# A hybrid decoder step: history products queued behind the adding transfers, the pooling group's newest columns ahead of VectorE's difference, two pooling products earlier

## Chip, core and metric

The kernel runs on one core of one Trainium2 chip. The metric is device time in microseconds (us), the median of several executions. All five engines of the core are used: TensorE (PE in the profile; PEld is its weight load), VectorE (DVE), ScalarE (ACT), GpSimd (POOL) and SyncE (SP, which only issues transfers).

## What is computed

One inference step of one hybrid layer on 288 token columns: 256 columns of a new sequence (the prompt) and 8 x 4 new columns of running requests (the samples). All in float32, channels on the partitions.

```
h    = RMSNorm(x)                                  # D_MODEL = 2048
a, gate, z = split(h @ w_in + b_in)                # 1024 columns each
u    = a * sigmoid(gate)
c    = silu(LayerNorm(depthwise_conv31(history ++ u)))
d    = windowed_mean(history ++ z) - z             # windows 2, 4, 8, 16, one for each of 4 groups
p    = (d @ pool_w, per group) * pool_scale
x   += concat(c, p) @ w_out
x   += relu(RMSNorm(x) @ w_ff1)^2 @ w_ff2          # D_FF = 8192
y    = RMSNorm(x)
```

The outputs are y for prompt and samples and the new convolution and pooling histories.

## The kernel before, in words

**Split products.** Every matrix product is made of three TensorE passes. A weight tile `wr` (128 x 1024 float32, 512 KB) is loaded, ScalarE rounds it to `whi` (line 260), and the rest `wlo = wr - whi` is made in one of three ways, which the table `WAYS` (line 73) deals out in turn: "V" on VectorE (line 265), "G" on GpSimd in two halves (line 268), and "D" by a transfer: ScalarE writes `-whi` into `wlo` (line 262), and a DMA issued from GpSimd's queue adds the weight to it straight from memory (line 263). These are the adding transfers; there are seven, in the stages that the code calls c3, c4, p3 and c5. The activations are split the same way (`hx`, `dx`, `mx`, `ax`, `fx`). A weight tile serves 24 matmuls; five pairs of `whi`, `wlo` buffers rotate, so a tile's cast waits for TensorE to be done with the tile five before it.

**Stages.** `SEQUENCE` (line 45) sets the order of the work on TensorE: eight convolution blocks c0 to c7 (128 channels of a and gate each, 96 matmuls of 128x128 on 128x288), four input blocks of the pooling groups p3 to p0, and the small pooling products P3 to P0 (12 matmuls each, line 498, into the accumulator `pp`). Then comes the output projection w0 to w7, first over the pooling half and then over the convolution half, and last the two feed-forward products, which take most of the time.

**Beside TensorE.** When a convolution block's accumulator is full, `conv_pair` (lines 426 to 461) scales it on VectorE (line 432), makes the gate on ScalarE (line 434) and u on VectorE (line 436). The 31 taps of the prompt columns are a chain of VectorE instructions (line 448); two blocks' chains alternate. The taps of the sample columns are one GpSimd product per block over the history windows (line 451, tile `prd`, 128 x 992 elements, the history product) and one VectorE reduction (line 453). These are recorded with a late priority, so a scheduler lays them into the gaps that it sees. It sets each engine's order once, when the program is built; on the chip every engine takes its queue strictly in that order.

For a pooling group, `pool_group` (lines 465 to 491) scales the accumulator on VectorE (line 470, tile `tz`), adds the bias on ScalarE into `z_all`, makes running sums `s` on GpSimd by doubling (line 479), corrects the first sums (line 483), and forms `d`: VectorE for the 256 prompt columns (line 484), then GpSimd for the 32 newest, sample columns, a scaling of `s` in place (line 486) and a difference (line 487). ScalarE rounds d to `dx` hi (line 489) and VectorE makes `dx` lo (line 490). The pooling products read both.

**Orders written out by hand.** In a matmul group, each pair of row blocks gives six matmuls: four with hi activations (two with `whi`, two with `wlo`), then two with lo activations. `classes` (line 317) can deal the first matmuls of a group out in another order; the string `TURN` (line 70) is given to c2, c5, the start of w0 and some later groups. `between` (line 324) puts something into a group: in c7 the products P1 stand in front of row block 12 of 16, and in the shared group of w0 and w1 the products P0 stand in front of pair (0, 2), that is behind 36 matmuls.

Of the kernel before, what the change touches and what calls it, by code (L numbers as in the profile page):

```python
# [12 lines left out]
ALU = mybir.AluOpType  # L13
# [3 lines left out]
P = 128  # L17
D = 2048
SEQ = 256
NB, NS = 8, 4  # L20
# [4 lines left out]
CW = 31  # L25
# [61 lines left out]
def trunk_kernel(ctx: ExitStack, tc: tile.TileContext, io):  # L87
# [46 lines left out]
    def f32(t):  # L134
        return t.bitcast(F32)
# [113 lines left out]
        last = mm(psum[:, 0, :T], minus, total, start=True, stop=True)  # L249
        return row_of(psum, psum[:, 0, :T], *args), last  # L250

    turns = {}

    def split_part(raw, src, hi, lo, way):

        nc.scalar.copy(hi, raw)  # L260
        if way == "D":
            nc.scalar.activation(lo, f32(hi), AF.Copy, scale=-1.0)
            nc.gpsimd.dma_start(lo, src, accum_op=ALU.add)
        elif way == "V":
            nc.vector.tensor_tensor(lo, raw, f32(hi), op=ALU.subtract)  # L265
        else:
            for j in range(0, raw.shape[1], 2):
                nc.gpsimd.tensor_tensor(lo[:, j : j + 2, :], raw[:, j : j + 2, :], f32(hi[:, j : j + 2, :]), op=ALU.subtract)  # L268

    def spl():  # L270
        return [wspl.tile([P, 4, 256], F32R, name=nm("w" + part), tag="w" + part) for part in ("hi", "lo")]
# [140 lines left out]
    rb = row("rb")  # L412


    cs, pcs = [], []
    sum_c = tmpp.tile([P, 2, T], F32, name="sum_c", tag="ag2", bufs=2)

    def history(i):
# [8 lines left out]
    def conv_pair(i, banks):  # L427
        up = u_all[:, i, 0:UO]
        us = samples(u_all[:, i, UO:UL], US)
        ta, gate = [b[:, :T] for b in banks]  # L430
        for b in (gate, ta):
            nc.vector.tensor_tensor(b, b, rb, op=ALU.mult)
        tg = tmpp.tile([P, 2, T], F32, name=nm("tg"), tag="ag", bufs=2)[:, 0, :]
        nc.scalar.activation(tg, gate, AF.Sigmoid, bias=v("b_in", 8 + i))
        for out, a, b in ((up[:, CH:UO], ta[:, :SEQ], tg[:, :SEQ]), (us[:, :, CH:US], samples(ta[:, SEQ:T], NS), samples(tg[:, SEQ:T], NS))):
            nc.vector.scalar_tensor_tensor(out=out, in0=a, scalar=v("b_in", i), in1=b, op0=ALU.add, op1=ALU.mult)
        if i % 2 == 0:
            cs.append(actp.tile([P, 2, T], F32, name=nm("c"), tag="c", bufs=4))
        c = cs[i // 2][:, i % 2, :]
        with later():  # L440
            if i % 2 == 0:
                pcs.append(cvp.tile([P, 2, SEQ], F32, name=nm("pc"), tag="cv"))
            pc = pcs[i // 2][:, i % 2, :]
            cwv = vec[:, CWO + i * CW : CWO + (i + 1) * CW]
            nc.scalar.activation(pc, up[:, 0:SEQ], AF.Identity, bias=v("conv_b", i), scale=cwv[:, 0:1])  # L445
            for w in range(1, CW):
                dst = pc if w < CW - 1 else c[:, 0:SEQ]
                nc.vector.scalar_tensor_tensor(out=dst, in0=up[:, w : w + SEQ], scalar=cwv[:, w : w + 1], in1=pc, op0=ALU.mult, op1=ALU.add)  # L448
            prd = prdp.tile([P, NB, NS, CW + 1], F32, name=nm("prd"), tag="prd")
            nc.scalar.activation(prd[:, :, :, CW], ones[:, 0 : NB * NS].rearrange("p (b t) -> p b t", t=NS), AF.Identity, bias=v("conv_b", i), scale=0.0)  # L450
            nc.gpsimd.tensor_tensor(prd[:, :, :, 0:CW], windows(us, CW), cwv[:, None, None, :].to_broadcast([P, NB, NS, CW]), op=ALU.mult)  # L451
            cso = c[:, SEQ:T]
            nc.vector.tensor_reduce(samples(cso, NS), prd, axis=AX.X, op=ALU.add)
            if i % 2 and 1 < i < N8 - 1:
                for m in range(2):
                    nc.gpsimd.tensor_tensor(sum_c[:, m, :], (cs[0] if i == 3 else sum_c)[:, m, :], cs[i // 2][:, m, :], op=ALU.add)
            if i == N8 - 2:
                for part in (sum_c[:, 1, :], c):
                    nc.gpsimd.tensor_tensor(sum_c[:, 0, :], sum_c[:, 0, :], part, op=ALU.add)
# [4 lines left out]
    def pool_group(g):  # L464
        nc.sync.dma_start(z_all[:, 2 * g : 2 * g + 2, ZO:ZL], io["hist_p"][:, 2 * g : 2 * g + 2, :])
        bk = bank2()
        gemm(each(bk), hx)
        z = z_all[:, 2 * g : 2 * g + 2, :]
        tz = tmpp.tile([P, 2, T], F32, name=nm("tz"), tag="ag", bufs=2)
        nc.vector.tensor_tensor(tz, bk[:, :, :T], both(rb), op=ALU.mult)  # L470
        for m in range(2):
            b_in = v("b_in", 16 + 2 * g + m)
            nc.scalar.activation(z[:, m, PH:ZO], tz[:, m, 0:SEQ], AF.Identity, bias=b_in)
            nc.scalar.activation(samples(z[:, m, ZO:ZL], ZS)[:, :, PH:ZS], samples(tz[:, m, SEQ:T], NS), AF.Identity, bias=b_in)
        s, w = z, 1
# [8 lines left out]
        nc.vector.scalar_tensor_tensor(out=d[:, :, 0:SEQ], in0=s[:, :, PH:ZO], scalar=1.0 / w, in1=z[:, :, PH:ZO], op0=ALU.mult, op1=ALU.subtract)  # L484
        news = [x[:, :, ZO:ZL].rearrange("p m (b t) -> p m b t", t=ZS)[:, :, :, PH:] for x in (s, z)]
        nc.gpsimd.tensor_scalar(news[0], news[0], 1.0 / w, None, op0=ALU.mult)
        nc.gpsimd.tensor_tensor(d[:, :, SEQ:T].rearrange("p m (b t) -> p m b t", t=NS), news[0], news[1], op=ALU.subtract)
        dh, dl = act2("dx", tag="p", bufs=4)
        nc.scalar.copy(dh, d)
        nc.vector.tensor_tensor(dl, d, f32(dh), op=ALU.subtract)  # L490
        dd[g] = dh, dl
# [33 lines left out]
    for kind, i in SEQUENCE[3:-1]:  # L525
        if (kind, i) == ("P", 1):
            continue
        if kind == "c":
            conv_pair(i, conv_products(i, classes=TURN if i == 5 else "", **(dict(gets=ahead(1), between={12: lambda: pool_products(1)}) if i == 7 else {})))
        elif kind == "p":  # L530
            pool_group(i)
        else:
            pool_products(i)
    proj = [halves(dd[k // 2])[k % 2] for k in korder]
    bks = [bank2() for _ in range(2)]
    both_gets = [ahead(1) for _ in range(2)]
    early = [(k, m) for k in (0, 2, 4) for m in range(4)]
    early.sort(key=lambda km: km[1] // 2)
    gemm(each(bks[0]) + each(bks[1]), proj, gets=[lambda k, m: both_gets[m // 2][0](k, m % 2)], between={(0, 2): lambda: pool_products(0)}, classes="." * 36 + TURN, pairs=early + [(6, m) for m in range(4)])
    chain.clear()  # L540
    load_table(AF.Abs_reciprocal_sqrt, f32(mixp[1][0])[:, 0:1])
    with later(2 * LATER):
# [239 lines left out]
```

## Time and profile before

| | |
|---|---|
| median of 3 runs | 1081.95 us (1081.67 to 1083.03) |
| the profiled execution's own time | 1082.43 us |
| its span, first to last instruction | 1080.6 us |
| busy: TensorE, VectorE, ScalarE, GpSimd | 1069.2, 633.7, 479.0, 175.9 us |
| matmuls | 8176 |
| granted TensorE clock | 0.998 |

The profile is of one execution. The 1.8 us between its time and its span lie outside the first and the last instruction. Times of day in the trace are microseconds from the span's start. GpSimd works almost only in the first 205 us, which hold the mixing part of the layer; the change touches nothing behind it. An engine's idle time is put down to whatever released it last.

### The profile page before, as it was taken

To read this page: it belongs to the slowest core of one execution; us is meant where nothing else is said; L and a number is where in the kernel's file an instruction comes from. 1 tells how busy PE (TensorE), PEld (TensorE's weight loads), DVE (VectorE), ACT (ScalarE), POOL (GpSimd) and SP (SyncE) were. 2 spreads that over 40 slices of the span, in tenths; PEclk is the share of its full clock that TensorE was granted. 3 is DMA by queue.
4 is the path that set the end of the run, shared out by engine and by line. 5 is a ranking of instruction groups with operands and counts; after the bars stand their busy time and mean duration, and the time that the engine had idled before them with its cause. 6 is when DMAs were issued, how large, how long until landed. Compare 5 with 4: busy or idle time off the path is not lost.

```text
span 1080.6 us, 19528 instructions
## 1 busy us (share of the span) xinstructions
PE 1069.2 (99%) x8176; PEld 1067.9 (99%) x8176; DVE 633.7 (59%) x810; ACT 479.0 (44%) x588; POOL 175.9 (16%) x182
## 2 busy tenths in 40 slices
PE   9999999999999999999999999999999999999996
PEld 8999999999999999999999999999999999999996
DVE  7899999788654544444554444555544445554553
ACT  8654445665544433334443333444433334444441
POOL 0878979512000000000000000000000000000001
PEclk9999999999999999999999999999999999999999
DMA  9896478555555555555555555555555555555522
GB/s 326 288 263 182 145 187 247 177 171 173 162 173 166 169 175 163 170 173 165 170 174 164 170 170 167 171 173 162 173 168 167 173 171 164 173 166 170 172 79 88
DMA packets 58296, 190.71 MB, mean 176 GB/s; under 512 B 6240, under 2 KB 11232, under 8 KB 58208
## 3 DMA queue, kind: packets, MB, share of 16 engines
q1 hardware_dynamic: 56336, 184.35, 54.3%
q0 software_dynamic: 1008, 3.67, 1.9%
q8 instruction: 64, 1.05, 0.4%
q10 hardware_dynamic: 864, 1.44, 0.4%
q14 instruction: 24, 0.20, 0.0%
HBM read 185.16 MB, written 4.28 MB: 175 GB/s over the span
## 4 chain that ended last, share of the span: by engine, by line
PE 75%; issue 21%; ACT 2%; POOL 1%; DMA 1%; SPq 0%; POOLq 0%; DVE 0%
PE ac L291 74%; POOL wlo L268 1%; DMA wr<-in_w 1%; ACT whi L349 1%; PE pp L291 1%; DMA wlo<-in_w 1%; ACT hx L354 0%; ACT z_all L405 0%; POOL prd L451 0%; POOL xT L718 0%; ACT whi L260 0%; SPq L191 0%; POOLq L768 0%; DVE xT L691 0%; ACT whi L356 0%
## 5 line engine op out<-in xcount | busy, mean ns | idle before, releaser
L260 ACT CAST whi<-wr 128x1024 fp32r<-128x1024 f32 (+1 forms) x332 | 346.5, 1044 | 551.3 <-PE ac L291 536.7
L265 DVE TENSOR_TENSOR wlo<-wr,whi 128x1024 fp32r<-128x1024 f32 x288 | 353.5, 1227 | 348.1 <-ACT whi L260 348.1
L291 PE MATMUL ac<-ax,whi 128*128 128x288 f32 x2048 | 351.0, 292 | 0.0
L291 PE MATMUL ac<-fx,whi 128*128 128x288 f32 x2048 | 350.2, 292 | 0.0
L291 PEld LDWEIGHTS ac<-ax,whi 128*128 128x128 f32 x2048 | 296.0, 187 | 0.0
L291 PEld LDWEIGHTS ac<-fx,whi 128*128 128x128 f32 x2048 | 295.6, 187 | 0.0
L291 PE MATMUL ac<-ax,wlo 128*128 128x288 f32 x1024 | 217.3, 292 | 0.0
L291 PE MATMUL ac<-fx,wlo 128*128 128x288 f32 x1024 | 216.4, 292 | 0.0
L291 PEld LDWEIGHTS ac<-ax,wlo 128*128 128x128 f32 x1024 | 162.5, 187 | 0.0
L291 PEld LDWEIGHTS ac<-fx,wlo 128*128 128x128 f32 x1024 | 162.2, 187 | 0.0
L291 PE MATMUL ac<-hx,whi 128*128 128x288 f32 x768 | 131.9, 296 | 1.4 <-DVE hx L352 1.4
L718 POOL TENSOR_TENSOR xT<-xT,rf 128x288 f32<-128x288 f32 x4 | 3.1, 795 | 799.9 <-ACT rf L722 799.9
L291 PEld LDWEIGHTS ac<-hx,whi 128*128 128x128 f32 x768 | 112.6, 190 | 1.8 <-ACT hx L354 1.7
L268 POOL TENSOR_TENSOR wlo<-wr,whi 128x512 fp32r<-128x512 f32 x74 | 102.4, 1433 | 17.1 <-ACT whi L260 16.0
L448 DVE SCALAR_TENSOR_TENSOR pc<-u_all,vec,pc 128x256 f32<-128x256 f32 x232 | 99.3, 479 | 1.9 <-ACT pc L445 0.7
L291 PE MATMUL ac<-hx,wlo 128*128 128x288 f32 x384 | 80.4, 295 | 0.2 <-DMA wlo<-in_w 0.2
L291 PEld LDWEIGHTS ac<-hx,wlo 128*128 128x128 f32 x384 | 61.1, 189 | 0.4 <-DMA wlo<-in_w 0.4
L291 PE MATMUL ac<-dx,whi 128*128 128x288 f32 x256 | 46.8, 295 | 0.0
L291 PE MATMUL ac<-mx,whi 128*128 128x288 f32 x256 | 44.9, 293 | 0.0
L660 DVE SCALAR_TENSOR_TENSOR t<-ac,r 128x576 f32<-128x576 f32 x32 | 24.2, 757 | 25.4 <-PE ac L291 25.3
L291 PEld LDWEIGHTS ac<-dx,whi 128*128 128x128 f32 x256 | 38.4, 188 | 0.2
L291 PEld LDWEIGHTS ac<-mx,whi 128*128 128x128 f32 x256 | 37.5, 188 | 0.2 <-DVE xT L579 0.2
(129 smaller groups left out, 529.6 us busy)
## 6 DMA issues: line engine op xcount, KB each, us to landing
wr<-in_w SPq DMA_DIRECT2D x335, 512.0 KB, 3.8
wlo<-in_w POOLq DMA_DIRECT2D x7, 512.0 KB, 7.8
xT<-in_xT SPq DMA_DIRECT2D x8, 288.0 KB, 7.7
wr<-in_w SPq DMA_DIRECT2D x5, 256.0 KB, 3.9
out_u_out<-u_all SPq DMA_DIRECT2D x1, 1208.0 KB, 9.6
u_all<-in_hist_c SPq DMA_DIRECT2D x8, 136.0 KB, 5.3
out_z_out<-z_all SPq DMA_DIRECT2D x1, 668.0 KB, 9.2
z_all<-in_hist_p SPq DMA_DIRECT2D x4, 152.0 KB, 6.6
```

The costliest lines, as they stand in the source:

```text
L260: nc.scalar.copy(hi, raw)
L265: nc.vector.tensor_tensor(lo, raw, f32(hi), op=ALU.subtract)
L268: nc.gpsimd.tensor_tensor(lo[:, j : j + 2, :], raw[:, j : j + 2, :], f32(hi[:, j : j + 2, :]), op=ALU.subtract)
L291: last = nc.tensor.matmul(*args, **kw)
L349: nc.scalar.copy(hi[:, blocks[0]], raw[:, blocks[0]])
L448: nc.vector.scalar_tensor_tensor(out=dst, in0=up[:, w : w + SEQ], scalar=cwv[:, w : w + 1], in1=pc, op0=ALU.mult, op1=ALU.add)
L660: nc.vector.scalar_tensor_tensor(out=t, in0=bk[:, :, :T], scalar=0.0, in1=both(rows2[0]), op0=ALU.max, op1=ALU.mult)
L718: eng.tensor_tensor(xk, xk, r[:, None, :].to_broadcast([P, n, T]), op=ALU.mult)
```

## The change

Four edits, all of them on the order of work; every operation, its size and its count stay.

1. The history product of a block is recorded so that it stands behind an adding transfer in GpSimd's queue: blocks 0 and 1 behind the first transfer, block 2 behind the second, blocks 3 and up behind the fourth. For this the taps of blocks 2 and 3 are recorded one block later.
2. In a pooling group GpSimd's two operations on the newest columns are recorded ahead of VectorE's difference. They work in place on `s`, so before, the scaling had to wait for VectorE to have read it.
3. From c7 on, the weight differences on GpSimd stand behind group 1's newest columns, and those of the output projection behind group 0's.
4. P1 goes in front of row block 8 of c7 instead of 12 (24 matmuls sooner), and P0 in front of pair (4, 0), behind 24 matmuls instead of 36. `TURN` follows P0 as before.

```diff
-            nc.gpsimd.dma_start(lo, src, accum_op=ALU.add)
+            added.append(nc.gpsimd.dma_start(lo, src, accum_op=ALU.add))
...
-                nc.gpsimd.tensor_tensor(lo[:, j : j + 2, :], raw[:, j : j + 2, :], f32(hi[:, j : j + 2, :]), op=ALU.subtract)
+                with tc.issue_after(pooled[-1].ins) if pooled else nullcontext():
+                    nc.gpsimd.tensor_tensor(lo[:, j : j + 2, :], raw[:, j : j + 2, :], f32(hi[:, j : j + 2, :]), op=ALU.subtract)
...
+        while waiting:
+            taps(*waiting.pop())
+        if i in (2, 3):
+            waiting.append((i, up, us))
+        else:
+            taps(i, up, us)
...
-            nc.gpsimd.tensor_tensor(prd[:, :, :, 0:CW], windows(us, CW), cwv[:, None, None, :].to_broadcast([P, NB, NS, CW]), op=ALU.mult)
+            with tc.issue_after(added[max(0, min(3, 2 * i - 3))].ins):
+                nc.gpsimd.tensor_tensor(prd[:, :, :, 0:CW], windows(us, CW), cwv[:, None, None, :].to_broadcast([P, NB, NS, CW]), op=ALU.mult)
...
-        nc.vector.scalar_tensor_tensor(out=d[:, :, 0:SEQ], in0=s[:, :, PH:ZO], scalar=1.0 / w, in1=z[:, :, PH:ZO], op0=ALU.mult, op1=ALU.subtract)
...
-        nc.gpsimd.tensor_tensor(d[:, :, SEQ:T].rearrange("p m (b t) -> p m b t", t=NS), news[0], news[1], op=ALU.subtract)
+        last = nc.gpsimd.tensor_tensor(d[:, :, SEQ:T].rearrange("p m (b t) -> p m b t", t=NS), news[0], news[1], op=ALU.subtract)
+        newest[g] = last
+        nc.vector.scalar_tensor_tensor(out=d[:, :, 0:SEQ], in0=s[:, :, PH:ZO], scalar=1.0 / w, in1=z[:, :, PH:ZO], op0=ALU.mult, op1=ALU.subtract)
...
+        if i == 7:
+            pooled.append(newest[1])
-            ... between={12: lambda: pool_products(1)} ...
+            ... between={8: lambda: pool_products(1)} ...
...
+    pooled.append(newest[0])
-    gemm(..., between={(0, 2): lambda: pool_products(0)}, classes="." * 36 + TURN, ...)
+    gemm(..., between={4: lambda: pool_products(0)}, classes="." * 24 + TURN, ...)
```

Two places show what this does to the queues. First GpSimd's queue around the first adding transfer, in stage c3: `wlo_609` is the tile that the transfer adds to, the two `prd` are the history products of blocks 0 and 1, the other `wlo` are weight differences of c2 and c3. Before:

```order
L268 TENSOR_TENSOR wlo_604<-wr_599,whi_603 128x512 x2
L451 TENSOR_TENSOR prd_667<-u_all,vec 128x32x31
L451 TENSOR_TENSOR prd_708<-u_all,vec 128x32x31
L263 DMA wlo_609<-in_w 128x1024
L268 TENSOR_TENSOR wlo_618<-wr_613,whi_617 128x512 x2
```

And now:

```order
L269 TENSOR_TENSOR wlo_604<-wr_599,whi_603 128x512 x2
L263 DMA wlo_609<-in_w 128x1024
L462 TENSOR_TENSOR prd_667<-u_all,vec 128x32x31
L462 TENSOR_TENSOR prd_708<-u_all,vec 128x32x31
L269 TENSOR_TENSOR wlo_618<-wr_613,whi_617 128x512 x2
```

The transfer now leaves ahead of both products. The second and the fourth transfer change places with one product each in the same way.

The other place is VectorE's queue around the difference of pooling group 1 (`d_1868`, its lo part `dx_1873`), which P1 reads. The `pc` rows are taps, the `wlo` rows weight differences, `tz_2023` is the next group's scaling. Before, with `tz_2023` in the row right ahead of these:

```order
L484 SCALAR_TENSOR_TENSOR d_1868<-s_1865,z_all 128x2x256
L448 SCALAR_TENSOR_TENSOR pc_1057<-u_all,vec,pc_1057 128x256
L448 SCALAR_TENSOR_TENSOR pc_1714<-u_all,vec,pc_1714 128x256
L265 TENSOR_TENSOR wlo_2064<-wr_2056,whi_2063 128x1024
L448 SCALAR_TENSOR_TENSOR pc_1057<-u_all,vec,pc_1057 128x256
L448 SCALAR_TENSOR_TENSOR pc_1714<-u_all,vec,pc_1714 128x256
L265 TENSOR_TENSOR wlo_2157<-wr_2154,whi_2156 128x512
L448 SCALAR_TENSOR_TENSOR pc_1057<-u_all,vec,pc_1057 128x256
L448 SCALAR_TENSOR_TENSOR pc_1714<-u_all,vec,pc_1714 128x256
L448 SCALAR_TENSOR_TENSOR pc_1057<-u_all,vec,pc_1057 128x256
L448 SCALAR_TENSOR_TENSOR pc_1714<-u_all,vec,pc_1714 128x256
L490 TENSOR_TENSOR dx_1873<-d_1868,dx_1873 128x2x288
```

And now:

```order
L499 SCALAR_TENSOR_TENSOR d_1868<-s_1865,z_all 128x2x256
L458 SCALAR_TENSOR_TENSOR pc_1057<-u_all,vec,pc_1057 128x256
L458 SCALAR_TENSOR_TENSOR pc_1714<-u_all,vec,pc_1714 128x256
L458 SCALAR_TENSOR_TENSOR pc_1057<-u_all,vec,pc_1057 128x256
L458 SCALAR_TENSOR_TENSOR pc_1714<-u_all,vec,pc_1714 128x256
L458 SCALAR_TENSOR_TENSOR pc_1057<-u_all,vec,pc_1057 128x256
L502 TENSOR_TENSOR dx_1873<-d_1868,dx_1873 128x2x288
L458 SCALAR_TENSOR_TENSOR pc_1714<-u_all,vec,pc_1714 128x256
L458 SCALAR_TENSOR_TENSOR pc_1057<-u_all,vec,pc_1057 128x256
L481 TENSOR_TENSOR tz_2023<-ac_1920,rb_250 128x576
L458 SCALAR_TENSOR_TENSOR pc_1714<-u_all,vec,pc_1714 128x256
L458 SCALAR_TENSOR_TENSOR pc_1057<-u_all,vec,pc_1057 128x256
```

Between the difference and its lo part stand five taps, where eight taps and two weight differences stood; `tz_2023`, ahead of both before, and the weight differences now follow. Counted from the second result of P2 (line 502, `dx_1536`), 26 taps, `tz_2023` and two weight differences stood ahead of `dx_1873`; now 11 taps do.

On TensorE the 12 matmuls of P1 and the 12 of P0 move as edit 4 says, and nothing else does but the dealing by `TURN` behind P0, which now begins one pair earlier.

More of the change, by code (lines that the diff above doesn't have):

```diff
@@ L250, in row_of_sums @@
         return row_of(psum, psum[:, 0, :T], *args), last
-    turns = {}
+    turns, added, newest, pooled = {}, [], {}, []
     def split_part(raw, src, hi, lo, way):
@@ L412, in trunk_kernel @@
     rb = row("rb")
-    cs, pcs = [], []
+    cs, pcs, waiting = [], [], []
     sum_c = tmpp.tile([P, 2, T], F32, name="sum_c", tag="ag2", bufs=2)
@@ L438, in conv_pair, with taps @@
             cs.append(actp.tile([P, 2, T], F32, name=nm("c"), tag="c", bufs=4))
+        while waiting:
[4 more added lines that the diff above has]
+            taps(i, up, us)
+    def taps(i, up, us):
         c = cs[i // 2][:, i % 2, :]
@@ L527, in trunk_kernel @@
             continue
+        if i == 7:
+            pooled.append(newest[1])
         if kind == "c":
-            conv_pair(i, conv_products(i, classes=TURN if i == 5 else "", **(dict(gets=ahead(1), between={12: lambda: pool_products(1)}) if i == 7 else {})))
+            conv_pair(i, conv_products(i, classes=TURN if i == 5 else "", **(dict(gets=ahead(1), between={8: lambda: pool_products(1)}) if i == 7 else {})))
         elif kind == "p":
@@ L538, in trunk_kernel @@
     early.sort(key=lambda km: km[1] // 2)
-    gemm(each(bks[0]) + each(bks[1]), proj, gets=[lambda k, m: both_gets[m // 2][0](k, m % 2)], between={(0, 2): lambda: pool_products(0)}, classes="." * 36 + TURN, pairs=early + [(6, m) for m in range(4)])
+    gemm(each(bks[0]) + each(bks[1]), proj, gets=[lambda k, m: both_gets[m // 2][0](k, m % 2)], between={4: lambda: pool_products(0)}, classes="." * 24 + TURN, pairs=early + [(6, m) for m in range(4)])
     chain.clear()
```

## The prediction

> **What bounds the kernel now.** I read the page first, then who TensorE waits for, then its timeline around the waits.
>
> ```profile
> PE 1069.2 (99%) x8176; PEld 1067.9 (99%) x8176; DVE 633.7 (59%) x810; ACT 479.0 (44%) x588; POOL 175.9 (16%) x182
> ```
>
> ```profile
> PE ac L291 <- DVE hx L352: 1.4, 1, 1.4
> PE ac L291 <- DMA wlo<-in_w: 0.2, 1, 0.2
> ```
>
> TensorE is the bound, and the list of its waits is nearly empty: 1.4 us at the start, which the change does not reach, and one wait for an adding transfer. The change cannot shorten TensorE's work; all it can win is what TensorE loses between matmuls. The timeline of TensorE around that one wait (start, length, what, how many) shows more than the 0.2 us of the list:
>
> ```profile
> 47.99 0.68 PE L291 MATMUL ac<-hx,whi 128*128 128x288 f32 x4
> ...
> 48.77 0.68 PE L291 MATMUL ac<-hx,whi 128*128 128x288 f32 x4
> ...
> 49.55 0.68 PE L291 MATMUL ac<-hx,whi 128*128 128x288 f32 x4
> 50.42 0.54 PE L291 MATMUL ac<-hx,wlo 128*128 128x288 f32 x2 [0.20 <-DMA wlo<-in_w]
> 50.80 0.69 PE L291 MATMUL ac<-hx,whi 128*128 128x288 f32 x4
> ...
> 52.39 0.70 PE L291 MATMUL ac<-hx,whi 128*128 128x288 f32 x4
> ...
> 53.19 0.70 PE L291 MATMUL ac<-hx,whi 128*128 128x288 f32 x4
> ```
>
> Ahead of the wait six matmuls take 0.78 us (48.77 to 49.55), 130 ns each. Four of these from 49.55 should bring the next at 50.07; it came at 50.42, 0.35 late. The two behind it took 0.38 instead of 0.26, another 0.12. And from there six take 0.80 (52.39 to 53.19), 133.3 ns each. That lasts until c5, where the order `TURN` breaks the pattern of four and two:
>
> ```profile
> 85.19 0.56 PE L291 MATMUL ac<-hx,whi 128*128 128x288 f32 x3
> ```
>
> The windows show the slow stretch and a later one at a full clock (the columns: stretch, length, busy and matmuls, granted clock, DMA share, GB/s):
>
> ```profile
> 51.00:84.00 33.00, 33.00 (x250) 1.00 0.95 256
> 95.00:128.00 33.00, 33.00 (x256) 1.00 0.49 152
> ```
>
> Six matmuls fewer in 33 us. Is the slower spacing the wait's doing? A second place says so: later TensorE waits a little once more (a group of four takes 0.90 instead of 0.68), and again six take 0.80 behind it.
>
> ```profile
> 219.19 0.90 PE L291 MATMUL ac<-mx,whi 128*128 128x288 f32 x4
> ...
> 220.19 0.69 PE L291 MATMUL ac<-mx,whi 128*128 128x288 f32 x4
> ...
> 220.99 0.70 PE L291 MATMUL ac<-mx,whi 128*128 128x288 f32 x4
> ```
>
> **The first adding transfer leaves earlier.** GpSimd's and ScalarE's timelines, and the transfer in the chain of waits:
>
> ```profile
> 38.90 1.30 POOL L268 TENSOR_TENSOR wlo<-wr,whi 128x512 fp32r<-128x512 f32 x1
> 40.16 4.33 POOL L451 TENSOR_TENSOR prd<-u_all,vec 128x992 f32<-128x992 f32 x2
> 44.41 1.01 POOL L263 DMA_DIRECT2D wlo<-in_w  x1
> ```
>
> ```profile
> 39.26 1.06 ACT L262 ACTIVATE wlo<-whi 128x1024 fp32r<-128x1024 f32 x1
> ```
>
> ```profile
> 44.41 5.97 DMA wlo<-in_w
> ```
>
> What the transfer needs, ScalarE's negated tile, is ready at 40.32 and GpSimd's difference ahead of it ends at 40.20; it then stands behind two history products for 4.1 us. Ahead of them it leaves at about 40.4 and, with the same 5.97 us, lands at 46.4, against 50.07 when TensorE wants it: 3.7 us to spare. So the wait goes. Gain: 0.35 + 0.12, and the slow spacing from 50.80 to 85.2: 34.4 / 0.1333 = 258 matmuls at 3.3 ns, 0.86. Sum **1.33 us**.
>
> [...]
>
> The moved products cost: both wait for the transfer's issue, at most 1.0 us of GpSimd, and end that much later than before. Behind them on GpSimd stand c3's weight differences, which start no later, since issue and products only change places. VectorE, in strict order, reaches its two reductions and waits there for some 1 us in all, with the taps and c2's scaling queued behind. VectorE's cover is its own wait for TensorE:
>
> ```profile
> DVE ac L432 <- PE ac L291: 2.5, 3, 1.3
> ```
>
> Three waits, 2.5 us in all, the longest 1.3. I cost it at nothing; without that cover it would be 1 us of taps, late on an engine that TensorE does not wait for until the layer norm.
>
> **The later adding transfers come close.** Once TensorE is faster, the next transfers are due sooner. By 76 us it is 0.47 + 0.63 = 1.1 us early, by 79 us 1.18. The tightest are the fourth and the fifth, in stage p3: issue, time to landing, and the weight load that needs the tile.
>
> ```profile
> 63.76 2.16 POOL L451 TENSOR_TENSOR prd<-u_all,vec 128x992 f32<-128x992 f32 x1
> 65.99 0.88 POOL L263 DMA_DIRECT2D wlo<-in_w  x1
> 68.90 0.87 POOL L263 DMA_DIRECT2D wlo<-in_w  x1 [2.04 <-ACT wlo L262]
> ```
>
> ```profile
> wlo<-in_w POOLq DMA_DIRECT2D x1, 512.0 KB, 9.8
> ```
>
> ```profile
> wlo<-in_w POOLq DMA_DIRECT2D x1, 512.0 KB, 10.2
> ```
>
> ```profile
> 75.99 0.32 PEld L291 LDWEIGHTS ac<-hx,wlo 128*128 128x128 f32 x2
> ```
>
> ```profile
> 79.19 0.32 PEld L291 LDWEIGHTS ac<-hx,wlo 128*128 128x128 f32 x2
> ```
>
> ```profile
> 64.38 1.06 ACT L262 ACTIVATE wlo<-whi 128x1024 fp32r<-128x1024 f32 x1
> ```
>
> The fourth lands at 65.99 + 9.8 = 75.8, wanted at 75.99; the fifth at 68.90 + 10.2 = 79.1, wanted at 79.19. Hardly any room. The fourth no longer stands behind a history product (63.76 to 65.92): its negated tile is ready at 65.44, and that cast is paced by TensorE, 0.8 us earlier, so it leaves at about 64.9, 1.1 us sooner, and keeps its 0.2 us. The fifth waits for ScalarE, 0.86 us earlier by the same pacing, while it is due 1.18 earlier: short by 0.2 if it still takes 10.2 us. But the 10.2 are a queue: the two land 3.3 us apart, and the one ahead starts 1.1 us sooner. Bounds: no wait at all, or a landing that does not move (79.1 against 78.0), a wait of 1.1 us with 0.12 and some 45 slow matmuls (0.15) behind it, which eats the gain. I take none, since both the queue ahead and the issue move forward, and keep 0 to 1.3 for the range.
>
> **The pooling part.** P1 is wanted 24 matmuls, 3.12 us, sooner, and TensorE is 1.33 us early. Its fifth matmul reads the lo part:
>
> ```profile
> 160.94 0.68 PE L291 MATMUL pp<-dx,whi 128*128 128x288 f32 x4
> ```
>
> ```profile
> 148.60 3.22 DVE L448 SCALAR_TENSOR_TENSOR pc<-u_all,vec,pc 128x256 f32<-128x256 f32 x8
> ...
> 152.41 1.35 DVE L484 SCALAR_TENSOR_TENSOR d<-s,z_all 128x512 f32<-128x512 f32 x1
> ...
> 154.47 1.69 DVE L265 TENSOR_TENSOR wlo<-wr,whi 128x1024 fp32r<-128x1024 f32 x1
> ...
> 159.03 0.75 DVE L490 TENSOR_TENSOR dx<-d,dx 128x576 fp32r<-128x576 f32 x1
> ```
>
> ```profile
> 156.87 0.86 POOL L487 TENSOR_TENSOR d<-s,z_all 128x64 f32<-128x64 f32 x1
> ```
>
> Before, it ended at 159.78, wanted at 160.94. Now it is wanted at 156.5, so it must come 3.3 us sooner. Since P2's second result 15 taps at about 0.39 (3.22 for 8, overlapping by 0.08) and two weight differences, the larger 1.6, no longer stand ahead of it: at least 7.5 us less. The rows printed around it account for three taps and the larger difference, 2.8 us, with the smaller one and `tz` on top, and VectorE is packed here, so fewer rows ahead is sooner. What else it needs, GpSimd's newest columns, stood behind weight differences until 157.73 and now stands ahead of them. That puts three small operations, the largest 0.86 here, at most 2.6 us, in front of GpSimd's weight tiles for c7:
>
> ```profile
> 145.50 5.05 POOL L268 TENSOR_TENSOR wlo<-wr,whi 128x512 fp32r<-128x512 f32 x4
> ```
>
> ```profile
> 151.19 0.32 PEld L291 LDWEIGHTS ac<-hx,wlo 128*128 128x128 f32 x2
> ```
>
> The first of these two tiles is done halfway, at 148.0, and wanted at 151.19: 3.2 us, and since their casts are paced by TensorE, its earliness does not shorten that. The cover holds; without it the loss would be what is late, 2.6 at most. Nothing is won on TensorE by being sooner either: gain and cost nothing. P0 reads its lo part in the same way:
>
> ```profile
> 170.30 0.68 PE L291 MATMUL pp<-dx,whi 128*128 128x288 f32 x4
> ```
>
> ```profile
> 165.42 0.74 DVE L490 TENSOR_TENSOR dx<-d,dx 128x576 fp32r<-128x576 f32 x1
> ```
>
> It ended at 166.16 (165.42 and 0.74) and was wanted at 170.30. It is now wanted 1.56 (12 matmuls) and 1.33 sooner, which leaves 1.2 us even if VectorE gains nothing.
>
> **The sum.** The profiled execution took 1082.43, 1.8 more than its span and 0.48 over the median of the three runs, 1081.95. 1082.43 - 1.33 = 1081.10 for such an execution, and 1081.95 - 1.33 = **1080.6** for the median.
>
> **Rivals.**
>
> (1) A later adding transfer takes over the wait. For it: the 0.1 to 0.2 us of room; against: it leaves sooner. Typically a wait of 0.25 with 0.27 behind it: 1080.6 + 0.5 = 1081.1; at the bound 1081.9. Chance 0.22.
>
> (2) [...] Chance 0.10.
>
> (3) P1 becomes the wait, and the kernel slower. If VectorE's lo part of group 1 stays where it was in time, because ScalarE or GpSimd hold up its difference and all taps behind it, TensorE stands 3.3 us at P1, then 0.12, then runs slow for about 84 matmuls until `TURN` (0.28): +3.7 - 1.33 = 2.4, 1084.3. It decides when VectorE moves forward by less than 3.3 us; the rows printed around it give 2.8 and a little more, the whole count 7.5. Chance 0.06.
>
> (4) The wait stays: the landing hangs on the DMA engines rather than on the issue (share 0.95 in that stretch). Against: 4 us sooner. 1081.95. Chance 0.04.
>
> (5) The short wait at 219 us goes as well, as everything ahead of it shifts: another 0.22 and, if the slow spacing there lasts 10 us, 75 matmuls at 3.3 ns (0.25): 1080.1. Nothing in the change is aimed there. Chance 0.06.
>
> The forecast keeps 0.52.
>
> **How the numbers follow.** From 1079.9 (rival 5, and 0.2 of spread between medians) to 1082.2 (rivals 1 and 4 at their bound, and 0.25 of the same spread) lie all cases but rival 3 and tails. About 0.2% (2.2 us) is what a measurement of this kernel tells from no change. Faster by more than that needs over 2.2 us, more than the forecast and rival 5 together (1.8): 0.04. Slower by that much is rival 3: 0.06. Within: 0.90.
>
> **What would show it.** Right: the transfer leaves at about 40.4, TensorE's list has no wait for `wlo`, six matmuls take 0.78 from 43 to 85 us, the window 51 to 84 holds 256 matmuls, c7 starts 1.3 us sooner, and P1 follows without a gap. Wrong: a wait for `wlo` at 75 to 79 us (rival 1), 0.80 for six without a wait ahead of it (rival 2), a wait for `dx` at 156 (rival 3).

## The result and the profile after

| | median of its runs | ratio to before, 95% interval |
|---|---|---|
| before | 1082.35 us (7 runs) | |
| changed | 1085.95 us (7 runs) | 1.0031 [1.0021, 1.0042] |

The kernel became slower by 3.6 us, more than the 0.2% that the prediction set as the bound. The profiled execution took 1085.72 us, its span is 1084.0.

**The first adding transfer did what was forecast.** GpSimd's timeline shows it leaving at 40.75 (it stood at 44.41), and TensorE's timeline runs through the place of the old wait without a gap, six matmuls in 0.78 us (start, length, what, how many):

```profile
40.75 1.05 POOL L263 DMA_DIRECT2D wlo<-in_w  x1 [0.74 <-POOL wlo L269]
```

```profile
49.35 0.68 PE L292 MATMUL ac<-hx,whi 128*128 128x288 f32 x4
...
50.13 0.68 PE L292 MATMUL ac<-hx,whi 128*128 128x288 f32 x4
...
61.83 0.68 PE L292 MATMUL ac<-hx,whi 128*128 128x288 f32 x4
62.58 0.53 PE L292 MATMUL ac<-hx,wlo 128*128 128x288 f32 x2
62.95 0.69 PE L292 MATMUL ac<-hx,whi 128*128 128x288 f32 x4
...
63.74 0.70 PE L292 MATMUL ac<-hx,whi 128*128 128x288 f32 x4
```

Two things in the lower rows: at 62.58 a new gap. The four matmuls from 61.83 should bring the next at 62.35; it came 0.23 late and two more took 0.37 instead of 0.26. It is the second adding transfer, which I had not worked out, and behind it the spacing is slow again (62.95 to 63.74: six in 0.79 to 0.80).

**The loss is at 165 us.** TensorE's timeline there, then the granted clock in two windows (stretch, length, busy and matmuls, clock, DMA share, GB/s):

```profile
164.45 0.42 PE L292 MATMUL ac<-dx,whi 128*128 128x288 f32 x2
167.00 0.53 PE L292 MATMUL ac<-dx,wlo 128*128 128x288 f32 x2 [2.12 <-DVE wlo L265]
167.37 0.69 PE L292 MATMUL ac<-dx,whi 128*128 128x288 f32 x4
...
168.23 1.16 PE L292 MATMUL ac<-dx,whi 128*128 128x288 f32 x4
169.19 0.68 PE L292 MATMUL ac<-dx,wlo 128*128 128x288 f32 x2
```

```profile
164.60:168.00 3.40, 1.27 (x10) 1.00 0.79 145
168.10:171.40 3.30, 3.30 (x16) 0.50 0.98 382
```

TensorE stands from 164.7 to 167.0 for the first weight tile of w0 (way "V", line 265); two matmuls take 0.26, so 2.29 are lost. Then the clock is at 0.50 for 3.4 us: four matmuls take 0.96 (168.23 to 169.19), 240 ns each, and with some 14 of them another 1.5 us go. 2.29 + 0.11 (the two behind the wait) + 1.5 = 3.9. Against that stand 0.45 us won between 46 and 151 us, and 0.2 by which this execution started up sooner. Net 3.25; the two profiled executions differ by 3.29. The profiled execution has two such stretches at half clock, the other at its start (7.6 us), and a mean clock of 0.995. Three of the seven executions have 0.997, by the same count room for only one, so the 1.5 us need not be in each of them.

The late tile itself, on VectorE's timeline after and before:

```profile
165.72 1.23 DVE L265 TENSOR_TENSOR wlo<-wr,whi 128x1024 fp32r<-128x1024 f32 x1
```

```profile
163.00 1.28 DVE L265 TENSOR_TENSOR wlo<-wr,whi 128x1024 fp32r<-128x1024 f32 x1
```

**Why VectorE is late.** VectorE's and GpSimd's timelines in stage p0, after and, below, before:

```profile
133.81 2.29 DVE L265 TENSOR_TENSOR wlo<-wr,whi 128x1024 fp32r<-128x1024 f32 x1
...
137.97 2.22 DVE L265 TENSOR_TENSOR wlo<-wr,whi 128x1024 fp32r<-128x1024 f32 x1
```

```profile
132.46 2.55 POOL L269 TENSOR_TENSOR wlo<-wr,whi 128x512 fp32r<-128x512 f32 x2
137.83 3.52 POOL L269 TENSOR_TENSOR wlo<-wr,whi 128x512 fp32r<-128x512 f32 x2 [2.82 <-ACT whi L260]
```

```profile
133.53 1.21 DVE L265 TENSOR_TENSOR wlo<-wr,whi 128x1024 fp32r<-128x1024 f32 x1
...
136.23 1.21 DVE L265 TENSOR_TENSOR wlo<-wr,whi 128x1024 fp32r<-128x1024 f32 x1
```

```profile
131.76 4.13 POOL L268 TENSOR_TENSOR wlo<-wr,whi 128x512 fp32r<-128x512 f32 x2
```

The same differences took 1.21 us before and 2.29 and 2.22 after. GpSimd's pair that began at 132.46 ends at 135.01; VectorE's difference, begun at 133.81, ends at 136.10: 1.09 behind GpSimd's end, about its own length. It stood until GpSimd had finished. Before, VectorE's difference had the turn, and it was GpSimd that paid (4.13 for two halves that take 2.55 alone). The starts that decide are close: in the pair at 138 us GpSimd's half began at 137.83 and VectorE's difference at 137.97. The Trainium skill describes this in "SBUF — State Buffer", section Who interferes with whom: VectorE with two SBUF inputs and a GpSimd operation that reads SBUF exclude each other for a whole instruction, and whichever issues first has it. These rows agree. VectorE has no idle time from 124.1 to 174.7 us, so nothing takes up what it loses.

### The profile page after: what moved, and what is told of

It reads as the page before. It is cut to its first block, busy times and chain, and to the rows that moved or that the text cites. A ratio compares the mean times of both kernels' runs of the same rounds, so it can differ in the third digit from the quotient of the medians.

```text
span 1084.0 us, 19533 instructions
## 1 busy us (share of the span) xinstructions
PE 1070.1 (99%) x8176; PEld 1068.6 (99%) x8176; DVE 637.1 (59%) x810; ACT 478.7 (44%) x588; POOL 177.4 (16%) x182
## 4 chain that ended last, share of the span: by engine, by line
PE 70%; issue 21%; DVE 4%; POOL 4%; DMA 1%; ACT 0%; POOLq 0%
PE ac L292 70%; DVE pc L458 2%; POOL wlo L269 2%; POOL s L490 1%; DMA wlo<-in_w 1%; DVE wlo L265 1%; DMA wr<-in_w 0%; DVE d L499 0%; POOL xT L733 0%; POOL prd L462 0%; DVE dx L502 0%; PE pp L292 0%; ACT whi L260 0%; DVE dx L514 0%; DVE c L464 0%
```

## The experiments

Two numbers are used throughout. "Nine operations" is the sum of the durations of nine VectorE operations with two SBUF inputs, in their order of before: the difference of group 2, P2's weights, the lo part of group 2, two differences of p0, P1's weights, difference and lo part of group 1, c7's difference (0.69 + 0.82 + 0.99 + 1.21 + 1.21 + 0.83 + 1.35 + 0.75 + 1.69 = 9.54 us before, 13.19 after). "Lost" is how much later than before matmul 1300 of the profile (177 us) starts, less the same for matmul 1100 (151 us). Both are read from the one profiled execution of each kernel. The last column is the median less that of before, timed beside it.

| kernel | nine operations | lost, 151 to 177 us | median against before |
|---|---|---|---|
| before | 9.54 | 0 | |
| the whole change | 13.19 | 3.99 | +3.6 |
| edit 1 alone | 11.80 | 3.07 | +3.3 |
| edits 2 and 3 alone | 11.26 | 2.79 | +4.0 |
| edit 4 alone | 9.55 | 2.41 | +2.5 |
| whole, w0 in order of use | 13.23 | 2.37 | +3.4 |
| whole, VectorE first | 10.06 | 0.00 | +0.75 |
| whole, VectorE first, second transfer sooner | 10.05 | 0.01 | +0.24 |
| edit 1, one product moved | 11.76 | 3.06 | +3.3 |
| edit 1, VectorE first | 10.71 | 1.34 | +1.3 |

**The edits one by one.** First the three parts, each on the kernel before; the diffs are the hunks of the change.

> Edit 1 alone (the history products behind the adding transfers; pooling order, P1 and P0 as before). Theory A (the loss is the first weight tile of w0, made too late on VectorE because edits 2 and 3 set VectorE's and GpSimd's operations against each other): no wait for that tile, the wait of 50 us gone, the wait for the second adding transfer at 62.5 us in its place: 0.2 to 1.0 us faster than before. Theory B (edit 4 makes it late, P1's results standing ahead of the tile): the same. Theory C (edit 1 makes it late: TensorE is due sooner and VectorE waits for the delayed history products): a wait for the tile at 164 us, 1 us or more, and 2 to 4 us slower than before.

> Edits 2 and 3 alone (newest columns ahead of VectorE's difference, weight differences of c7 and w behind them; history products, P1 and P0 as before). Theory A: the first tile of w0 comes 1 to 2.5 us late, and VectorE's two-input differences between 124 and 160 us take up to 2.3 us where GpSimd's are in their way: 1 to 4 us slower than before. Theories B and C: the tile is in time, within 0.5 us of before.

> Edit 4 alone (P1 and P0 sooner; the queues of the pooling group as before). All theories: TensorE wants group 1's lo part at about 157.8 us and gets it at 159.8, so a wait of some 2 us for dx at P1. Theory B: a wait for the first tile of w0 beside it or behind it. Theory A and C: none for the tile beyond what P1's wait covers (TensorE is 2 us later itself): 2 us slower than before, 3.5 if the clock halves behind the wait.

Measured: edit 1 alone 1085.55 us (ratio 1.0028 [1.0017, 1.0039]), edits 2 and 3 alone 1086.21 (1.0033 [1.0022, 1.0044]), edit 4 alone 1084.72 (1.0022 [1.0014, 1.0031]). Each part alone is slower, by 9.8 us in sum, the whole by 3.6: the losses do not add. TensorE's waits behind 60 us, of edit 1, of edits 2 and 3, and of edit 4:

```profile
PE ac L291 <- DVE dx L512: 0.8, 1, 0.8
PE pp L291 <- DVE dx L500: 0.5, 1, 0.5
PE pp L291 <- ACT dx L499: 0.3, 1, 0.3
```

```profile
PE ac L292 <- DVE wlo L265: 2.0, 1, 2.0
```

```profile
159.24 0.53 PE L291 MATMUL pp<-dx,whi 128*128 128x288 f32 x2 [1.01 <-ACT dx L489]
...
160.58 0.80 PE L291 MATMUL pp<-dx,whi 128*128 128x288 f32 x4 [0.54 <-DVE dx L490]
```

Edits 2 and 3 bring the late tile of w0 (theory A), and two waits for adding transfers at 76 and 80 us beside it, 1.1 us, which I did not follow up. Edit 1 alone has no wait for that tile, but three others: VectorE is late, and what pays is whatever TensorE wants next. Theory A had this part at a gain, so A as I had put it fell. Theory C had its time right (2 to 4 us slower), but put it at w0's tile, for which this kernel does not wait. Edit 4 alone is a plain wait at P1, with none for w0's tile, so theory B fell; its nine operations are as before. In edit 1 alone the excess sits here:

```profile
124.39 1.76 DVE L494 SCALAR_TENSOR_TENSOR d<-s,z_all 128x512 f32<-128x512 f32 x1 [0.32 <-POOL s L493]
130.03 2.59 DVE L500 TENSOR_TENSOR dx<-d,dx 128x576 fp32r<-128x576 f32 x1
```

0.69 and 0.75 are their least. That gave theory A': VectorE is the second bound of this stretch, and its meetings with GpSimd, which any new order deals out anew, land on TensorE.

**w0's tiles in the order of use.** TensorE wants the second half of w0's weights first; here they are split in that order.

```diff
-        for raw, src in halves:
+        for raw, src in halves[::-1] if stage == "w0" else halves:
...
+        if stage == "w0":
+            parts.reverse()
```

> The whole change, but the two weight tiles of w0 are cast and split in the order in which TensorE reads them, the first wanted first (as it stands, the second half of the weights is wanted 8 us ahead of the first half and made behind it). Theory A, B and C alike say that the wait at 165 us is all of the loss: the first tile is ready at about 164.6 instead of 166.9, wanted at 164.6: no wait or one under 0.3 us, no half clock behind it, 3.5 to 4 us faster than the whole change, 0 to 0.8 us faster than before. If the half clock has another cause than the wait, 1.5 us of the loss stays.

Measured 1085.6 us (1.003 [1.002, 1.004]); against the whole change no gain. The wait for the tile is gone, and others stand in its place:

```profile
PE pp L294 <- DVE dx L516: 1.0, 1, 1.0
...
PE ac L294 <- DVE u_all L439: 0.7, 1, 0.7
PE ac L294 <- DVE xT L596: 0.6, 1, 0.6
```

All name VectorE; the first is P0, which waits until VectorE has read the accumulator `pp` for the results of P1. The expectation failed because it looked at one tile, not at the queue behind it.

**VectorE goes first.** One-column writes of VectorE into the tile, overwritten at once, make GpSimd's half wait until VectorE's difference is done. It is done for three halves of p0; the order of both queues is otherwise the changed one.

```diff
+            def behind_vector(j):
+                with tc.issue_after(differences[-1].ins):
+                    nc.vector.memset(f32(lo)[:, j, 0:1], 0.0)
+                half(j)
```

> The whole change, with three halves of GpSimd's weight differences in stage p0 made to wait for VectorE's difference beside them, by a one-column write of VectorE into the tile. Theory A': the two differences of VectorE that took 2.28 and 2.22 us take 1.2, VectorE is 2 us sooner from there, and the first tile of w0 is late by 0.4 us or not at all: 1082 to 1083, 3 us faster than the whole change, if no other meeting takes the place of the two. Rival (the long durations are a matter of the record, or of memory traffic): durations and time stay as in the whole change.

Measured 1082.86 us (1.0007 [0.9998, 1.0015]): 2.9 us of the 3.6 are back. VectorE, GpSimd and TensorE:

```profile
134.04 1.22 DVE L265 TENSOR_TENSOR wlo<-wr,whi 128x1024 fp32r<-128x1024 f32 x1
...
137.15 1.22 DVE L265 TENSOR_TENSOR wlo<-wr,whi 128x1024 fp32r<-128x1024 f32 x1
```

```profile
135.36 1.29 POOL L269 TENSOR_TENSOR wlo<-wr,whi 128x512 fp32r<-128x512 f32 x1 [1.36 <-DVE wlo L273]
```

```profile
164.67 0.42 PE L305 MATMUL ac<-dx,whi 128*128 128x288 f32 x2
164.93 0.42 PE L305 MATMUL ac<-dx,wlo 128*128 128x288 f32 x2
```

The two differences take 1.22, GpSimd waits 1.36 in their stead and can afford it, and TensorE goes through w0's first tile without a gap. Up to 205 us its trace has GpSimd's and ScalarE's operations in the changed kernel's order, and VectorE's too but for the three writes, so the new order alone, without the lost turns, does not make the tile late. This is the run that shows the cause of the loss in the whole change.

**Room for VectorE.** Three kernels hold back the last 21 taps of block 5 and the last 10 of block 6 until VectorE has made w0's tiles: the whole change, before, and before with only the first transfer moved.

```diff
+HELD = {5: 21, 6: 10}
...
-            for w in range(1, CW):
+            for w in range(1, CW - HELD.get(i, 0)):
```

> The whole change, with the last 21 taps of block 5 and the last 10 of block 6 held back behind VectorE's differences for w0 (all of them still computed, and nothing else moved): 8 taps fewer stand ahead of the tiles of w0. Theory A' (VectorE, which has no idle time from 124 to 185 us, is the second bound of this stretch, and what it loses to GpSimd's operations lands on TensorE): the first tile of w0 comes 3 us sooner, no wait over 0.3 us between 150 and 190 us, no half clock: about 1081.7, 4 us faster than the whole change and 0.3 to 1 us faster than before. Rival (the loss lies in ScalarE's or GpSimd's order and only shows on VectorE): the wait stays, within 1 us of the whole change.

> The kernel before with the same taps held back. Theory A': TensorE waits for nothing there before, so nothing to win: within 0.5 us of before. It is the yardstick for the whole change with held taps: their difference is what edit 1 wins at the first adding transfer, 0.5 to 1.3 us. Rival: if held taps themselves help TensorE in another way, this one gets faster as well.

> Before, with blocks 0 and 1's history products behind the first adding transfer and nothing else of the change (blocks 2 and up as before, no pooling edits, P1 and P0 as before), and the taps held back. The wait at 50 us goes, the second transfer leaves at 54.9 as before and is wanted 0.5 us sooner, at 62.7: a wait of 0.3 to 0.6 us there. Theory A': VectorE has room for its meetings with GpSimd, so no wait over 0.5 us from 150 to 190 us: 1081.3 to 1082.2. Rival: VectorE's order, which now differs from before's between 118 and 131 us, makes group 1's lo part 1 us late as with the whole of edit 1 alone: 1083 to 1085.

Measured 1093.48, 1090.12 and 1095.19 us (1.0103 [1.0089, 1.0117], 1.0073 [1.0061, 1.0086], 1.0116 [1.0101, 1.0131]). All three miss, for the yardstick fell too: the taps I took for free to wait are wanted by the layer norm. TensorE's wait there, with taps held in before:

```profile
PE pmean L293 <- DVE sum_c L572: 5.4, 1, 5.4
```

So VectorE has no room behind 165 us either. On A' these runs say little beyond that (the whole change still waited 0.7 for w0's tile). The third one tells something of edit 1: with only the first transfer moved, block 2's history product stays ahead of the second one.

```profile
64.95 0.54 PE L293 MATMUL ac<-hx,wlo 128*128 128x288 f32 x2 [2.40 <-DMA wlo<-in_w]
```

It leaves at 55.48 and TensorE waits 2.4 us: edit 1 does need its second part.

**The second transfer sooner.** GpSimd's halves of c4's first tile go behind the transfer. On the whole change with VectorE first:

> The whole change with VectorE going first in p0 (as in the kernel with the one-column writes), and the second adding transfer ahead of GpSimd's two halves of the weight tile before it (c4's first tile, which has 5 us to spare). The transfer left at 53.4 us and landed 9.3 us later, at 62.75, 0.36 us late. If the landing follows the issue, it leaves at about 52.1 (when ScalarE has negated the tile), lands at 61.5, and the wait of 0.36 us and the slow spacing behind it (some 170 matmuls at 3.3 ns, 0.56) go: 0.9 us faster than without this edit, 1082.0. If the landing hangs on the load of the DMA engines, it lands at 62.5 or later as before and nothing is won.

Measured 1082.21 us (1.0006 [0.9998, 1.0015]). GpSimd, and TensorE at the place:

```profile
51.97 0.87 POOL L263 DMA_DIRECT2D wlo<-in_w  x1 [1.48 <-ACT wlo L262]
```

```profile
61.95 0.68 PE L308 MATMUL ac<-hx,whi 128*128 128x288 f32 x4
62.47 0.42 PE L308 MATMUL ac<-hx,wlo 128*128 128x288 f32 x2
```

It left at 51.97, landed after 8.1 us, at 60.0, and the wait is gone. So the landing was not held at 62.5: beside the kernel with VectorE first alone (53.41 and 62.75) the transfer leaves 1.4 us sooner and lands 2.7 us sooner (0.7 of each is the earlier start of this execution). From matmul 300 to 1100, 46 to 151 us, this kernel wins 0.89 us on before, where the whole change wins 0.45. It gives 0.85 back behind 177 us, at a wait of 0.3 us for VectorE and slow spacing behind it; so does the kernel with VectorE first alone (0.88). Why that wait comes I did not settle. The intervals of the two kernels' times are nearly the same, so the 0.9 us expected between them is not shown by the times.

**Edit 1 alone again.** First one product, block 6's, made to wait for the lo part that took 2.59 us; then that with the second transfer sooner; then, with the product recorded behind P2, two places at once; and that with the second transfer sooner.

```diff
+                with tc.issue_after(low[2].ins):
+                    nc.vector.memset(prd[:, 0, 0, 0:1], 0.0)
```

> Edit 1 alone, with block 6's history product made to wait for VectorE's lo part of group 2 (by a one-column write), which took 2.59 us there where 0.75 is its least. Theory A' (edit 1 loses because it changes where VectorE and GpSimd meet): VectorE is 1.8 us sooner from 131 us, the waits of 160 to 174 us, 3.1 us together, shrink to 1.3 or less: 1082.0 to 1083.6. Rival (the delayed history products themselves hold VectorE up): as edit 1 alone, 1085.5.

> As the one before, with the second adding transfer ahead of the two halves of c4's first tile as well. If both theories hold: 0.9 us faster than that one, and the waits of 50 and 62 us both gone: 1081.1 to 1082.7. If the landing hangs on the load of the DMA engines: as the one before.

> Edit 1 alone, with VectorE going first at two places: GpSimd's first half of the last tile of p1 waits for VectorE's difference of group 2, and block 6's history product is recorded behind P2 and waits for VectorE's second tile of p0 (one-column writes again). Theory A' (edit 1 loses by where VectorE and GpSimd meet): group 2's difference and lo part and p0's two differences take 0.7, 0.75, 1.2 and at most 1.8 us, VectorE is 2 to 2.9 us sooner at 140 us, and the waits of 160 to 175 us, 3.1 us in edit 1 alone, come down to 1 us or less: 1082.0 to 1083.5. Rival (the delayed history products and reductions): waits and time as in edit 1 alone, 1085.5.

> The same with the second adding transfer ahead of c4's first two halves on GpSimd: no wait at 50 nor at 62 us, 0.9 us faster than the one before if theory A' holds: 1081.1 to 1082.6, at best 1 us below before.

Measured 1085.28 (1.0029 [1.0018, 1.0041]), 1084.64 (1.0027 [1.0017, 1.0037]), 1083.38 (1.0014 [1.0005, 1.0023]) and 1083.15 us (1.001 [1.0001, 1.0019]). The first misses: the lo part took 0.75, but the product then met the next difference.

```profile
134.68 2.97 DVE L265 TENSOR_TENSOR wlo<-wr,whi 128x1024 fp32r<-128x1024 f32 x1
```

The third has both out of each other's way, and a column-write that came too late for the difference of group 2, since the half of the tile without that column went ahead:

```profile
124.33 1.76 DVE L512 SCALAR_TENSOR_TENSOR d<-s,z_all 128x512 f32<-128x512 f32 x1 [0.32 <-POOL s L511]
...
129.54 0.75 DVE L518 TENSOR_TENSOR dx<-d,dx 128x576 fp32r<-128x576 f32 x1
134.03 1.22 DVE L269 TENSOR_TENSOR wlo<-wr,whi 128x1024 fp32r<-128x1024 f32 x1
```

2.0 of edit 1's 3.3 us are back, so A' holds for the larger part of it; the last 1.3 I did not settle. The sooner second transfer brought 0.6 us and 0.2 here, less than the 0.9 expected, both inside the spread of the runs.

**GpSimd out of the way.** Its six weight tiles of p2, p1 and p0 made by adding transfers, in the whole change, edit 1, before, and the whole change with the second transfer sooner.

```diff
-"p": "GVVG"
+"p": "DVVD"
```

> The whole change, with the six weight tiles that GpSimd splits in stages p2, p1 and p0 made by adding transfers instead (ways DVVD for GVVG): GpSimd no longer works beside VectorE's differences there, ScalarE has six negations of 1.06 us more. Theory A' (meetings with GpSimd make VectorE late): VectorE's 128x1024 differences from 95 to 150 us take 1.2 to 1.5 us, no wait for w0's first tile, no half clock: 1081.5 to 1082.9, some 3.5 us faster than the whole change. Rival (the change's own order makes VectorE late): a wait of 1 us or more remains, 1084 or more. Against both: ScalarE may come late with a cast.

> Edit 1 alone with the same six tiles made by adding transfers. Theory A': the waits of 160 to 175 us (3.1 us together in edit 1 alone) shrink to 1 us or less: 1081.5 to 1083.0. Rival (the delayed history products and reductions hold VectorE up): 1084 or more.

> Before, with the same six tiles made by adding transfers. TensorE waits for nothing after 60 us there, so the time stays within 0.5 us of before; it would be slower if the negations or the transfers come late, and then the two above are to be read against it.

> The whole change with the six tiles made by adding transfers, and the second adding transfer ahead of c4's first two halves on GpSimd. Both losses of the change are answered: no wait at 62.5 and none at 165 us: 0.9 us faster than without the latter, 1080.6 to 1082.0, below before by up to 1.3 us.

Measured 1086.07 (1.0035 [1.0023, 1.0048]), 1086.43 (1.0039 [1.0025, 1.0052]), 1085.81 (1.0035 [1.0022, 1.0048]) and 1084.35 us (1.0027 [1.0017, 1.0037]). All missed, the yardstick too, and so they don't part the theories: the new transfers come late themselves (1.3 us of waits in the yardstick), and some of VectorE's differences are kept out for several of GpSimd's sums. From the first of these kernels, VectorE and GpSimd, and then the same difference in before:

```profile
89.71 3.72 DVE L265 TENSOR_TENSOR wlo<-wr,whi 128x1024 fp32r<-128x1024 f32 x1
```

```profile
88.61 2.05 POOL L490 TENSOR_TENSOR s<-z_all 128x422 f32<-128x422 f32 x2
90.31 3.86 POOL L490 TENSOR_TENSOR s<-s 128x420 f32<-128x420 f32 x3
```

```profile
89.91 1.42 DVE L265 TENSOR_TENSOR wlo<-wr,whi 128x1024 fp32r<-128x1024 f32 x1 [0.36 <-ACT whi L260]
```

The difference stood about 2.5 us, while GpSimd finished the sum under way and two more.

**The slow spacing.** `TURN` at the start of c4 as well, on before:

```diff
-classes=TURN if i == 5 else ""
+classes=TURN if i in (4, 5) else ""
```

> Before, with the order TURN at the start of c4 as well as c5: no operation more or less. If TURN ends the slow spacing that a short wait begins: six matmuls take 0.80 us from 50.8 to about 60 us and 0.78 from there to 85, 0.6 us faster than before. If it ends at 85 us for another reason (the DMA engines are less busy from there): 0.80 until 85 us and no gain. A wait for an adding transfer may come sooner where TensorE is.

Measured 1081.34 us (0.9994 [0.9985, 1.0003]), not to be told from before. The timeline in c3 and in c4:

```profile
52.51 0.70 PE L291 MATMUL ac<-hx,whi 128*128 128x288 f32 x4
...
53.30 0.70 PE L291 MATMUL ac<-hx,whi 128*128 128x288 f32 x4
...
68.37 0.68 PE L291 MATMUL ac<-hx,whi 128*128 128x288 f32 x4
...
69.15 0.68 PE L291 MATMUL ac<-hx,whi 128*128 128x288 f32 x4
...
80.47 0.70 PE L291 MATMUL ac<-hx,whi 128*128 128x288 f32 x4
...
81.27 0.70 PE L291 MATMUL ac<-hx,whi 128*128 128x288 f32 x4
```

0.79 to 0.80 behind the old wait, 0.78 behind the new `TURN` (at a DMA share of 0.99 to 1.00, against 0.90 ahead of it), and 0.80 again from about 75 us on. There the fourth transfer lands just when it is wanted, at 74.98, and at 78.5 TensorE waits for the fifth. So a short wait begins the slow spacing and `TURN` ends it; the DMA load does not. The gain is missing because what `TURN` wins by then, 0.28 us, is lost at these two transfers.

No kernel here beats both: three come to before's level (the two with VectorE first in the whole change, and this one), and their intervals all hold 1.

## Why the prediction was wrong

- **The first transfer's wait goes**: right. 40.75 against about 40.4; landed at 48.5, not 46.4, 7.8 us after its issue instead of 5.97, but still 1.3 us ahead of its need at 49.9.
- **The slow spacing goes with the wait**: right in kind. That it would stay without the wait fell: the spacing was 130 ns until the next wait and 133 behind it. But of the 0.86 only about 0.3 was won, since the second transfer began it anew and took 0.34 itself (0.23 and 0.11); 0.45 of the 1.33 came through.
- **"The tightest are the fourth and the fifth"**: wrong for the changed kernel, where both came in time (74.59 and 77.61). The second failed. It left at 53.31, 1.55 us sooner than before, and landed at 62.53, 0.17 sooner, no more than this execution started up sooner: 9.2 us on the way instead of 7.84. I had let the later landings move with the issue and had not worked out this one. It is rival 1 at another place, and accounts for the 0.9 us that are missing of the 1.33. The warning itself was sound: in the kernel with the second transfer sooner, TensorE is 1.08 us ahead at 75 us, the fourth and the fifth land as they are wanted (74.12 and 77.45), and 0.19 us and the fast spacing are lost there.
- **History products at nothing**: right for what it named: VectorE's three waits for them are 1.4 us, taken out of its waits for TensorE (1.2 us left of 2.5). What it didn't name, the new place of all that follows in VectorE's queue, cost 3.3 us in edit 1 alone.
- **"Gain and cost nothing" for the pooling part**: this is the step that failed. Between 151 and 177 us, where it put nothing, TensorE lost 3.99 us. P1 itself was in time, as forecast: its lo part ended at 155.36 (wanted at 157.17), 4.4 us sooner. The count of rows held from where it began: from P2's second result to this lo part it is 8.1 us less than before, and I had counted at least 7.5. But that result itself came 3.7 us later, and those six of the nine operations that stand ahead of it took 3.5 us more in sum. P0's margin of 1.2 was used up: its lo part ended at 167.61, 1.45 later than before, and the accumulator that P1's results must leave free, which I had not counted, is later still (a wait of 1.0 where w0's tile came in time). And the tile that stood between, w0's first, ready at 164.28 and wanted at 165.23 before, I did not look at. It came at 166.95.
- **The root**: "fewer rows ahead is sooner" took durations from the profile of before as if they belonged to the operations. For a VectorE operation with two SBUF inputs they belong to the meeting: 1.21 us alone and up to 2.97 behind one operation of GpSimd.
- **Rival 3** had the right sign and the wrong victim: VectorE held up by GpSimd, a wait of 2 to 3 us. It was given 0.06, for P1 alone. That its price of 2.4 is close to what edit 4 alone cost (2.5) is luck: the 2.4 has the 1.33 of gain taken off, which edit 4 alone does not have.
- The half clock behind a wait was in no case of mine: 1.5 of the 3.9 us.

## What to carry over

When a change deals out the order of two engines that exclude each other, count every pair of operations that can meet, not rows: an engine with no idle time for 50 us has as much margin as its tightest consumer, here 0.95 us, and two lost meetings eat it. Look for that tightest consumer along the whole queue behind the change, beyond the operations that the change names. And a wait of 2 to 3 us can cost more than its length: 2.3 us became 3.9 here.

## What the runs showed of the hardware

- A wait that fills most of one TensorE clock window brought half a clock for the next. The trace's records of the clock change 3.41 us apart. In the whole change TensorE stands for 2.3 us of one such window (164.63 to 168.04), and the clock is 0.50 in the next; in the whole change with transfers for GpSimd's tiles and the second transfer sooner, for 2.1 us of one, and the clock is 0.50 behind it. With edits 2 and 3 alone the wait is nearly as long, 2.1 us, but lies across a border, 1.0 and 1.1 us on the two sides, and the clock stays:

```profile
166.00:168.40 2.40, 0.43 (x4) 1.00 1.02 340
168.40:171.80 3.40, 3.40 (x26) 1.00 0.97 347
```

  So it does at a wait of 2.6 us, 1.4 and 1.2 on the two sides, in the kernel with only the first transfer moved. The Trainium skill, "TensorE: Matmul & The Clock Gate", section What's actually happening, has the free-running window of 3413 ns, which the records show, and half speed after an idle one. Here a window that was idle to three fifths was enough, and one that was idle to two fifths was not.
- A meeting of VectorE with GpSimd's sums can cost one sum or several. In before and in the changed kernel a difference of 1.21 us that met the sums of group 3 took 1.42 and 1.43 us: VectorE had its turn behind the sum under way. With the added transfers it took 3.72, as above. There the first sums stand right behind a transfer's issue, and in the record each begins 0.35 us before the one ahead of it ends, where in before it is 0.04. Why VectorE then waits for several is not shown.
- An adding transfer of 512 KB took 6.0 to 10.2 us in before, and up to 11.5 in edits 2 and 3 alone. The sooner issue of the second one moved its landing by 0.2 us (1.5 us sooner issued, in the changed kernel) or by 2.7 us (2.9 us sooner, with the two halves of c4 behind it), of which 0.2 and 0.9 are the earlier starts of these executions; what makes the difference is not shown.
